# Sums of quarter weights made by VectorE as fillers of the order, in place of accumulating transfers in DRAM

## Chip, cores and metric

The kernel runs on one core of a Trainium2 chip. The metric is the device time of one execution in microseconds. The core has five engines with queues of their own, which run side by side and wait for each other by semaphores: TensorE (PE, matmuls), VectorE (DVE), ScalarE (ACT), GpSimd (POOL) and SyncE (SP). In this kernel SP and POOL also issue the DMA transfers, SP the loads and the transposing transfers, POOL most stores. The on-chip memory SBUF has 128 partitions; matmul results go to PSUM; everything else lies in DRAM.

## What is computed

One layer of a hybrid encoder for two groups of requests, 1024 prompt rows and 8 x 16 sample rows, 1152 tokens together, with a model width of 1024:

```python
mod = jax.nn.silu(c) @ w_ada + b_ada
shift, scale, gate = jnp.split(mod[:, None, :], 3, axis=-1)
h = rms_norm(x, norm_g) * (1 + scale) + shift
proj = h @ w_in
q, k, v, z_att, z_ssd, xbc, dt_raw, gates = jnp.split(proj, IN_SPLITS, axis=-1)
...
o_att, k_st, v_st = attn_fn(q, k, v)
att_branch = (o_att.reshape(b, s, ATT_WIDTH) * jax.nn.silu(z_att)) @ w_att_proj
xbc, conv_new = causal_dwconv(xbc, conv_buf, conv_w, conv_b)
xbc = jax.nn.silu(xbc)
...
y, h_new = ssd_scan(xs_h, dt, a,
...
y = (y + d_skip.astype(jnp.float32)[:, None] * xs_h).reshape(b, s, SSD_WIDTH).astype(x.dtype)
y = y * jax.nn.silu(z_ssd)
y = rms_norm(y.reshape(b, s, SSD_GROUPS, SSD_WIDTH // SSD_GROUPS),
             ssd_norm_g.reshape(SSD_GROUPS, SSD_WIDTH // SSD_GROUPS)).reshape(b, s, SSD_WIDTH)
ssd_branch = y @ w_ssd_proj
g_att, g_ssd = jnp.split(gates, 2, axis=-1)
merged = jax.nn.sigmoid(g_att) * att_branch + jax.nn.sigmoid(g_ssd) * ssd_branch
out = x + gate * (merged @ w_out)
```

There is attention over a band of chunks with 16 heads, and a state-space branch with 32 heads of 64 in 4 groups, scanned in chunks. The scan is float32 in the reference.

## The kernel before

**Stages.** All activations lie with channels on partitions and the 1152 tokens (`NT`) along the free dimension. Float32 products are made from float16 halves: a weight block is loaded as float32 into a `raw` buffer (line 672), ScalarE makes its high half (L690), VectorE its low half (L691), ScalarE sums its squares (L682), and three matmuls per block (L949, L950, L952) take high x high, high x low and low x high. The program is a list of items: eight units of attention (pairs of heads), then 16 pairs of state-space heads in 4 groups, then the gates, the attention projection, the two state-space projections and the output projection. The dense products of the state-space items run on PE while the attention's last units are still worked off, so the two stages overlap for some 150 us.

**The state-space stage.** A pair's dense part makes x (through `conv_gen`: ScalarE moves the product out of PSUM at L1783 and L1786, VectorE runs the convolution at L1806 and the gate multiply at L1812) and z (ScalarE L1964, VectorE L1965). `prelude` broadcasts rows of `acs_d` and `eacs_d` over partitions (L1980, L1984, loads on SP), loads the state (L1986) and builds decays on ScalarE (L1992, L1996). `main` turns x by a transposing DMA (L2017), unpacks it (L2019), scales it (L2024), runs the chunk products on PE (L2039, L2067, L2074, L2087) and stores y (L2104). At the last pair of a group PE sums squares over channels (L1368), for which VectorE adds the last square at L2127.

**Seven products in place of eight.** The second half of the gates and all later projections use a scheme with 7 products of quarter blocks in place of 8 (`quad_dense`, matmuls at L858 to L860). For each such block of weights with quarters a11, a12, a21, a22 it needs four sums besides: a21+a22, a21+a11, and two that build on the first. There are 20 of these blocks ("quads"). Before, the sums of four quads at a time are made by transfers alone (`quad_sums`, lines 693 to 712): two copies from the weights into the tensor `sum_d` in DRAM (L699, L700, on SP), four transfers on POOL's queue that add a quarter to what lies in DRAM (L698), and two copies within `sum_d` (L706, L710, on SP). Each moves 1 MB. The five batches are started at pairs 5, 7, 9, 11 and 13 of the item list (`SUMS`). The sums are loaded at L672 as pieces of a quad's job, beginning at 1303.6 us of the profile.

**What sets the order.** Generators first emit the whole program with a clock of their own (`pause` lets that clock pass); memory is handed out from an arena by layouts (`set_layout`). Then the class `Order` simulates the engines by a table of costs and gives each engine its final order: at each step the engine that is free first takes, among the instructions whose inputs are there, preferably those that are there with a margin, the one that was emitted earliest; nothing more than 1200 instructions ahead of the oldest open one is taken. On the chip each engine runs its list strictly in that order, so an instruction whose input is late holds up all behind it.

The choice in `Order.run` is this line:

```python
            u = min(sure or can, key=lambda u: u["i"])
```

Of the kernel before, what the change touches and what calls it, by code (L numbers as in the profile page):

```python
# [16 lines left out]
P = 128  # L17
# [122 lines left out]
class Order:  # L140
# [4 lines left out]
    SAFE_DMA = 2500.0  # L145
    SAFE_SLOT = 500.0
    AHEAD = 1200

    def __init__(self, tc, instructions, pinned, cuts, slow):
        self.tc, self.slow = tc, slow  # L150
        self.list = [x for x in instructions if x.opcode != "TilePoolBoundary"]
        self.pinned, self.cuts = pinned, cuts

# [76 lines left out]
    def build(self):  # L230
# [54 lines left out]
        for u in units:  # L285
            costs = [self.cost(x) for x in u["ins"]]
            u["busy"] = sum(c for c, _ in costs)
            u["lat"] = u["busy"] - costs[-1][0] + costs[-1][1]
            u["dma"] = u["ins"][0].opcode == "DMACopy" or u["ins"][0].opcode.startswith("DmaTranspose")
        self.tiles = tiles  # L290
# [23 lines left out]
    def run(self):  # L314
# [34 lines left out]
        while n < len(units):  # L349
            best = None  # L350
            for e in engines:
                lane = 0.0
                for u in ready[e]:
                    r, u["sure"] = u["r"], u["safe"]
                    for name in u.get("opens", ()):
                        s = slots[self.tiles[name][0]]
                        need = sum(self.tiles[o][0] == self.tiles[name][0] for o in u["opens"])
                        r = max(r, sorted(s)[need - 1] if len(s) >= need else 1e18)
                        u["sure"] = max(u["sure"], r + self.SAFE_SLOT)
                    u["now"] = r  # L360
                c = [u["now"] for u in ready[e] if u["i"] < low + self.AHEAD]
                if not c or min(c) > 1e17:
                    continue
                t = max(free[e], min(c))
                if best is None or t < best[0]:
                    best = (t, e)
            assert best, ("no unit can go on", [(e, [(u["i"], u["ins"][0].name) for u in ready[e]][:4]) for e in engines])
            t, e = best
            can = [u for u in ready[e] if u["now"] <= t and u["i"] < low + self.AHEAD]
            sure = [u for u in can if u["sure"] <= t]  # L370
            u = min(sure or can, key=lambda u: u["i"])
            ready[e].remove(u)
# [12 lines left out]
            if e == "PE":  # L385
                g = u["key"][1]
                if key[0] not in (None, g):
                    t += 70
                key[0] = g
            if e == "PE":  # L390
                log.append((t, t - free[e], u))
            start[u["i"]], finish[u["i"]] = t, t + lat
            free[e] = t + busy
            order[e].append(u)
            for name in u.get("uses", ()):
                x = self.tiles[name]
# [24 lines left out]
def trunk_kernel(ctx: ExitStack, tc: tile.TileContext, h, again):  # L421
# [32 lines left out]
    for n, w in PARAMS:  # L454
# [23 lines left out]
    bmask2 = cst[:, C_BM2:C_BM2 + 2]  # L478

    HN = NT // 2  # L480
    NSLOT = 12
    H0 = fixed[0] + 3 * 1024
    W0 = H0 + 16 * HN
# [14 lines left out]
    L_SSD = arena.set_layout(Z0, [("X", 1, XW), ("R", 2, 1184), ("t", 8, 36), ("pad", 1, 576), ("T", 9, NT), ("Y", 1, 1184), ("H", 1, 1024),  # L498
                                  ("g", 3, G3)])
    L_SSD["T"] = L_SSD["T"] + arena.set_layout(V0, [("T", 4, NT)])["T"]  # L500
    L_HEAD = dict(L_SSD, T=[x for x in L_SSD["T"] if x[0] + x[1] <= Z0 + 7 * NT])
    L_TAIL = arena.set_layout(Z0, [("T", 17, NT)])
    assert Z0 + 17 * NT + 2 * 384 <= E0
# [116 lines left out]
    dma = nc.sync.dma_start  # L620

    store = nc.gpsimd.dma_start
    pinned, cuts, slow = set(), set(), set()
    pinning = [True]

    def late(x):
# [63 lines left out]
            keep(nc.scalar.activation(hi, x, AF.Copy, scale=scale))  # L690
            keep(nc.vector.scalar_tensor_tensor(lo, x, scale, hi, ALU.mult, ALU.subtract))  # L691

    def quad_sums(i):

        b, s = batches[i], sum_d[i].rearrange("q p (s c) -> s p q c", c=512)
        x = h["quad"][2 * b[0] + NPLAIN:2 * b[-1] + 2 + NPLAIN].rearrange("(q o) p (e c) -> o e p q c", o=2, e=2)
        (a11, a12), (a21, a22) = ([x[o, e] for e in range(2)] for o in range(2))
        add = lambda out, x: nc.gpsimd.dma_start(out, x, accum_op=ALU.add)  # L698
        dma(s[0], a21)  # L699
        dma(s[2], a21)  # L700
        yield from pause(30000)
        add(s[0], a22)
        yield from pause(15000)
        add(s[2], a11)
        yield from pause(15000)
        dma(s[1], s[0])  # L706
        yield from pause(25000)
        add(s[1], a11)
        yield from pause(30000)
        dma(s[3], s[1])  # L710
        yield from pause(25000)
        add(s[3], a12)

    def quad_split(i):

        if i not in wsplit:
            bufs = []
            try:
# [3 lines left out]
                for b in bufs:  # L722
                    b.free()
                raise
            col = lambda k, e: slice((4 * e + k) * P, (4 * e + k + 1) * P)
            pick = {0: (bufs[0], bufs[1], col, 0, 0), 1: (bufs[0], bufs[1], col, 1, 1), 2: (bufs[5], bufs[6], col, 1, 1),
                    3: (bufs[2], bufs[2], col, 0, 1), 4: (bufs[3], bufs[4], col, 0, 0), 5: (bufs[3], bufs[4], col, 1, 1),
                    6: (bufs[5], bufs[6], col, 0, 0)}

# [79 lines left out]
        job(*(h["wall"][1 + 4 * u + i] for i in range(3)))  # L809
        job(h["wall"][4 + 4 * u])  # L810
    job(*(h["wlast"][i] for i in range(4)))
    SUMS = (5, 7, 9, 11, 13)
    NPLAIN = 8
    gate_w, at = [], 29
    for g in range(NG):
# [8 lines left out]
    for i in range(NPLAIN):  # L824
        job(gate_w[i])
    NQ_G = (16 - NPLAIN) // 2
    batches = [range(0, NQ_G)] + [range(NQ_G + 4 * i, NQ_G + 4 * i + 4) for i in range(4)]
    sum_d = [drp.tile([len(b), P, 2048], F32, name=f"sum{i}_d") for i, b in enumerate(batches)]
    for i, b in enumerate(batches):
        for j, q in enumerate(b):  # L830
            job(h["quad"][2 * q + NPLAIN], h["quad"][2 * q + 1 + NPLAIN], sum_d[i][j][:, :1024], sum_d[i][j][:, 1024:], quad=True)

    HT = NT // 2
    HC = NT // 4
# [1598 lines left out]
    for p in range(NPAIR):  # L2433
        g = p // PPG
        if p % PPG == 0 and p:
            items.append((group_dense(g, L_SSD), [], [group_lat(g)], 0.5))
        items.append(ssd(p))
        if p in SUMS:
            items[-1][1].append(quad_sums(SUMS.index(p)))
    items.append((gates_dense(), [h_pieces(), att_prep()], [], 0.5))  # L2440
    items.append((att_dense(), [tile_loads(4, ("ga", gate_d, 0)), ssd_prep(), mod_gate()], [], 0.5))
    items.append((ssd_dense(0), [], [], 0.5))
    items.append((ssd_dense(1), [tile_loads(3, ("acc", acc_d, 0), ("gs", gate_d, 8), ("att", att_o, 0))], [], 0.5))
    items.append((out_dense(), [], [], 0.5))
    run(items)
    order = Order(tc, list(nc.cur_bb.bb.instructions), pinned, cuts, slow)
    order.build()
    order.run()
    order.apply()
# [1867 lines left out]
```

## Time and profile before

| | us |
|---|---|
| runs, median of 3 | 1773.9 (1771.29 to 1774.73) |
| profiled execution, its own time | 1774.65 |
| its span | 1772.6 |
| PE busy | 1691.9 |
| VectorE busy | 1331.4 |
| ScalarE busy | 1060.8 |
| POOL busy | 369.6 |
| granted PE clock, mean over the span | 0.988 |
| attention, with PE nearly always busy | about 50 to 540 |
| attention's tail beside the first state-space pairs | 540 to 700 |
| state-space pairs | 700 to about 1265 |
| projections with seven products | about 1265 to 1772 |

Span and times are those of one execution seen by the hardware profiler. A row of the table by stretches gives start and end of the stretch and its length, then for PE, PE's weight loads, VectorE, ScalarE and POOL the busy us and in brackets the number of instructions, then the granted PE clock (1.00 is full speed), the mean busy share of the 16 DMA engines (it can come out above 1) and GB/s. A row of the timeline gives start, duration, engine, line and operation; in square brackets stands how long the engine was idle before it and whose result ended that. SPq rows are what SP issued.

### The profile page before, as it was taken

What the parts mean: (1) busy time and instruction counts of PE and PEld (TensorE: products, weight loads), DVE (VectorE), ACT (ScalarE), POOL (GpSimd) and SP (SyncE); (2) the same over time, 40 slices, a digit from 0 to 9 for tenths busy, and PEclk for the clock granted to TensorE, in tenths of its full rate; (3) what the DMA queues carried; (4) which work ended last, traced back from release to release, by engine and by line L of the source; (5) the groups of instructions that cost most, each with busy time, mean ns of one, the idle gap of its engine ahead of it and who ended that gap; (6) DMA issues with size and microseconds to landing.
All of it is one profiled execution on the core that took longest, in us unless ns stands there. A gap on an engine that the chain in (4) does not pass through costs nothing.

```text
span 1772.6 us, 36471 instructions
## 1 busy us (share of the span) xinstructions
PE 1691.9 (95%) x14265; PEld 1127.0 (64%) x14265; DVE 1331.4 (75%) x2466; ACT 1060.8 (60%) x2130; POOL 369.6 (21%) x620
## 2 busy tenths in 40 slices
PE   7999999999999898999899899999999999999896
PEld 3556656556555455666566566766667777777674
DVE  6468677777775855969778797886798587879952
ACT  8766556556565446654846575575579575775540
POOL 0233323323243011212322231221231000000000
PEclk9999999999999999999999999999999999999998
DMA  9248778888989999998987663556557785786651
GB/s 382 70 125 209 199 203 206 209 200 202 217 242 211 243 230 219 251 249 234 239 241 178 181 181 116 151 150 182 171 180 265 265 296 196 246 302 232 219 182 56
DMA packets 308703, 369.13 MB, mean 208 GB/s; under 512 B 211037, under 2 KB 212457, under 8 KB 308521
## 3 DMA queue, kind: packets, MB, share of 16 engines
q1 hardware_dynamic: 286696, 307.65, 61.5%
q0 software_dynamic: 21824, 59.06, 13.0%
q8 instruction: 114, 1.87, 0.4%
q14 instruction: 69, 0.56, 0.1%
HBM read 265.05 MB, written 95.04 MB: 203 GB/s over the span
## 4 chain that ended last, share of the span: by engine, by line
PE 52%; DMA 14%; DVE 14%; ACT 12%; issue 6%; POOL 1%; SPq 0%; DVEq 0%; ACTq 0%; POOLq 0%
PE d L949 7%; PE d L952 7%; PE d L950 7%; PE d L1002 5%; PE d L1004 5%; PE d L1003 5%; DMA arena<-in_wall_dram 4%; ACT arena L682 2%; PE g L1608 2%; ACT arena L1992 2%; DVE arena L691 2%; DMA arena<-arena 2%; DVE arena L2179 2%; DMA arena<-acs_d 2%; DVE arena L1806 1%
## 5 line engine op out<-in xcount | busy, mean ns | idle before, releaser
L949 PE MATMUL d<-arena 128*128 128x384 f16 x1320 | 435.2, 330 | 9.0 <-DVE arena L1965 6.3
L952 PE MATMUL d<-arena 128*128 128x384 f16 x1320 | 434.1, 329 | 0.6 <-DVE arena L691 0.6
L950 PE MATMUL d<-arena 128*128 128x384 f16 x1320 | 434.2, 329 | 0.0
L682 ACT ACTIVATE arena<-arena 128x1024 bf16<-128x1024 f32 (+4 forms) x217 | 199.2, 918 | 177.5 <-DMA arena<-in_wall_dram 134.0
L691 DVE SCALAR_TENSOR_TENSOR arena<-arena 128x1024 f16<-128x1024 f32 (+2 forms) x157 | 181.3, 1162 | 57.1 <-ACT arena L690 56.7
L949 PEld LDWEIGHTS <-arena 128*128 128x128 f16 x1320 | 130.3, 99 | 93.7 <-issue 17.8
L690 ACT ACTIVATE arena<-arena 128x1024 f16<-128x1024 f32 (+2 forms) x157 | 155.0, 993 | 53.5 <-DMA arena<-sum_d 31.5
L1002 PE MATMUL d<-arena 128*128 128x384 f16 (+1 forms) x568 | 186.8, 329 | 0.0
L950 PEld LDWEIGHTS <-arena 128*128 128x128 f16 x1320 | 130.2, 99 | 88.6 <-issue 13.1
L952 PEld LDWEIGHTS <-arena 128*128 128x128 f16 x1320 | 130.2, 99 | 88.5 <-issue 3.5
L1004 PE MATMUL d<-arena 128*128 128x384 f16 (+1 forms) x568 | 186.1, 328 | 0.0
L1003 PE MATMUL d<-arena 128*128 128x384 f16 (+1 forms) x568 | 186.1, 328 | 0.0
L1548 ACT ACTIVATE arena<-arena 128x640 f32<-128x640 f32 (+4 forms) x144 | 100.8, 702 | 66.8 <-DVE arena L1551 66.4
L859 PEld LDWEIGHTS <-arena 128*128 128x128 f16 x1120 | 109.5, 98 | 40.4 <-issue 13.1
L858 PE MATMUL d<-arena 128*128 128x288 f16 x440 | 125.8, 286 | 3.8 <-ACT arena L877 3.1
L860 PEld LDWEIGHTS <-arena 128*128 128x128 f16 x1120 | 109.5, 98 | 30.6 <-issue 2.7
L858 PEld LDWEIGHTS <-arena 128*128 128x128 f16 x1120 | 109.7, 98 | 29.2 <-issue 1.7
L859 PE MATMUL d<-arena 128*128 128x288 f16 x440 | 125.8, 286 | 1.1 <-DVE arena L2179 1.1
L860 PE MATMUL d<-arena 128*128 128x288 f16 x440 | 125.8, 286 | 0.0
L858 PE MATMUL s<-arena 128*128 128x288 f16 x360 | 102.9, 286 | 4.2 <-ACT arena L877 2.5
L1806 DVE SCALAR_TENSOR_TENSOR arena<-arena 128x1176 f32<-128x1176 f32 x72 | 103.7, 1440 | 3.1 <-ACT arena L1803 2.2
L1992 ACT ACTIVATE arena<-arena 128x128 f32<-128x128 f32 x288 | 90.0, 391 | 22.0 <-DMA arena<-acs_d 22.0
(277 smaller groups left out, 3493.9 us busy)
## 6 DMA issues: line engine op xcount, KB each, us to landing
arena<-in_wall_dram SPq DMA_DIRECT2D x77, 512.0 KB, 5.3
sum_d<-in_quad_dram POOLq DMA_DIRECT2D x20, 1024.0 KB, 13.9
arena<-in_quad_dram SPq DMA_DIRECT2D x40, 512.0 KB, 4.2
arena<-sum_d SPq DMA_DIRECT2D x40, 512.0 KB, 4.2
arena<-acs_d SPq DMA_DIRECT2D x32, 576.0 KB, 5.6
arena<-in_kc_dram SPq DMA_DIRECT2D x64, 256.0 KB, 4.0
arena<-in_vc_dram SPq DMA_DIRECT2D x64, 256.0 KB, 4.1
arena<-in_wada_dram SPq DMA_DIRECT2D x24, 512.0 KB, 9.4
```

The source lines that it names most:

```text
L682: keep(nc.scalar.activation(junk[:, :n], x, AF.Square, scale=scale * n ** -0.5, accum_out=sums[:, c:c + 1]))
L690: keep(nc.scalar.activation(hi, x, AF.Copy, scale=scale))
L691: keep(nc.vector.scalar_tensor_tensor(lo, x, scale, hi, ALU.mult, ALU.subtract))
L858: nc.tensor.matmul(ps, wh, xh[:, c], start=first and k == 0, stop=False, skip_group_check=not first)
L859: nc.tensor.matmul(ps, wh, xl[:, c], start=False, stop=False, skip_group_check=not first)
L860: nc.tensor.matmul(ps, wl, xh[:, c], start=False, stop=k == 3, skip_group_check=not first)
L949: nc.tensor.matmul(ps, hi.r[:, wc], kh.r[:, tok], start=k == 0, stop=False)
L950: nc.tensor.matmul(ps, hi.r[:, wc], kl.r[:, tok], start=False, stop=False)
L952: nc.tensor.matmul(ps, lo.r[:, wc], kh.r[:, tok], start=False, stop=k == nk - 1)
L1002: nc.tensor.matmul(ps, kh.r[:, tok], wh, start=k == 0, stop=False)
L1003: nc.tensor.matmul(ps, kh.r[:, tok], wl, start=False, stop=False)
L1004: nc.tensor.matmul(ps, kl.r[:, tok], wh, start=False, stop=k == KT - 1)
```

## The change

`quad_sums` now handles one quad. It takes two buffers of 1024 float32 columns (layout `L_SUM`, two slots at the end of the stage's area, just behind those of the state-space layout), loads the quad's two halves from the weights, lets VectorE add quarters in place four times, and stores both buffers in pieces of 2 KB to a `sum_d` tensor of its own on POOL's queue. The weights' first half of each quad is packed with its two quarters swapped, and `quad_split` picks its parts accordingly. The 20 quads are handed evenly to pairs 0 to 14 of the item list. The four additions are marked as fillers: in `Order.run` they count as emitted 600 instructions later than they are, so that other work that is ready goes ahead of them.

```diff
+    FILL = 600
...
+            u["at"] = u["i"] + self.FILL * (u["ins"][0].name in self.fill)
...
-            u = min(sure or can, key=lambda u: u["i"])
+            u = min(sure or can, key=lambda u: u["at"])
...
+    NSUM = 2
...
+    L_SUM = arena.set_layout(E0 - NSUM * 1024, [("s", NSUM, 1024)])
...
-    def quad_sums(i):
-
-        b, s = batches[i], sum_d[i].rearrange("q p (s c) -> s p q c", c=512)
-        x = h["quad"][2 * b[0] + NPLAIN:2 * b[-1] + 2 + NPLAIN].rearrange("(q o) p (e c) -> o e p q c", o=2, e=2)
-        (a11, a12), (a21, a22) = ([x[o, e] for e in range(2)] for o in range(2))
-        add = lambda out, x: nc.gpsimd.dma_start(out, x, accum_op=ALU.add)
-        dma(s[0], a21)
-        dma(s[2], a21)
-        yield from pause(30000)
-        add(s[0], a22)
-        yield from pause(15000)
-        add(s[2], a11)
-        yield from pause(15000)
-        dma(s[1], s[0])
-        yield from pause(25000)
-        add(s[1], a11)
-        yield from pause(30000)
-        dma(s[3], s[1])
-        yield from pause(25000)
-        add(s[3], a12)
+    def quad_sums(q):
+
+        x = yield from wpair(L_SUM, "s", 1024)
+        for o, b in enumerate(x):
+            dma(b.ap, h["quad"][2 * q + NPLAIN + o])
+        yield from pause(7000)
+        a12, a11, a21, a22 = (b.ap[:, c:c + 512] for b in x for c in (0, 512))
+        for out, a, b in ((a22, a21, a22), (a21, a11, a21), (a11, a22, a11), (a12, a11, a12)):
+            fill.add(nc.vector.tensor_tensor(out, a, b, ALU.add).ins.name)
+            yield from pause(900)
+        s = sum_d[q].rearrange("p (s o c) -> p s o c", o=2, c=512)
+        for o, b in ((1, x[0]), (0, x[1])):
+            store(s[:, :, o], b.ap.rearrange("p (s c) -> p s c", c=512))
+        stored(*x)
...
-    SUMS = (5, 7, 9, 11, 13)
...
-        if p in SUMS:
-            items[-1][1].append(quad_sums(SUMS.index(p)))
+        items[-1][1].extend(quad_sums(q) for q in range(NQUAD * p // 15, min(NQUAD, NQUAD * (p + 1) // 15)))
...
+    ar["quad"][::2] = np.roll(ar["quad"][::2], 512, 2)
```

In the changed program a line behind `quad_sums` has a number that is lower by 4 (before L2019, now L2015), and the loading line L672 is L676.

SP's queue at the passage from attention to the state-space stage, before. `acs_d` and `eacs_d` hold the running sums of the scan, `in_wall` weights, `in_vc` cached values, `in_quad` the quads' weights:

```order
L1881 DMA acs_d<-arena 32x1152
L1884 DMA eacs_d<-arena 32x1152
L1590 DMA_TRANSPOSE arena<-arena 128x10x128 x2
L710 DMA sum_d<-sum_d 128x4x512
L1727 DMA arena<-in_vc_dram 128x512 x4
L1980 DMA arena<-acs_d 128x1152
L1590 DMA_TRANSPOSE arena<-arena 128x10x128 x2
L706 DMA sum_d<-sum_d 128x4x512
L672 DMA arena<-in_wall_dram 128x1024
```

The same place in the changed program:

```order
L1880 DMA eacs_d<-arena 32x1152
L1586 DMA_TRANSPOSE arena<-arena 128x10x128
L1723 DMA arena<-in_vc_dram 128x512 x3
L676 DMA arena<-in_wall_dram 128x1024
L1723 DMA arena<-in_vc_dram 128x512
L1976 DMA arena<-acs_d 128x1152
L701 DMA arena<-in_quad_dram 128x1024
L1586 DMA_TRANSPOSE arena<-arena 128x10x128 x2
L1773 DMA arena<-in_sconv_dram 128x24
```

The copies within `sum_d` are gone, and the first load of a quad (L701) stands here, behind the first broadcast of `acs_d`; no transfer of the sums stands ahead of it any more. (The previous `sum_d` transfers of SP stood before these rows, in the attention's last units.) The last load of a quad stands next to the load of the last pair's state.

VectorE's queue where the first quad is added, before. `arena` is SBUF, names that begin with d or g are PSUM tiles:

```order
L1806 SCALAR_TENSOR_TENSOR arena<-arena 128x1176
L2019 COPY arena<-arena 128x2x1152
L1812 SCALAR_TENSOR_TENSOR arena<-arena 128x1024
L1813 SCALAR_TENSOR_TENSOR arena<-arena 128x128
L2024 TENSOR_TENSOR arena<-arena 128x1152 x2
L1806 SCALAR_TENSOR_TENSOR arena<-arena 128x1176
L1965 SCALAR_TENSOR_TENSOR arena<-arena,d_8500 128x384
```

And in the changed program:

```order
L1802 SCALAR_TENSOR_TENSOR arena<-arena 128x1176
L2015 COPY arena<-arena 128x2x1152
L705 TENSOR_TENSOR arena<-arena 128x512
L1808 SCALAR_TENSOR_TENSOR arena<-arena 128x1024
L1809 SCALAR_TENSOR_TENSOR arena<-arena 128x128
L2020 TENSOR_TENSOR arena<-arena 128x1152 x2
L705 TENSOR_TENSOR arena<-arena 128x512 x2
L695 SCALAR_TENSOR_TENSOR arena<-arena 128x1024
L705 TENSOR_TENSOR arena<-arena 128x512
L1802 SCALAR_TENSOR_TENSOR arena<-arena 128x1176
```

The four additions (L705) stand singly or in pairs between the pair's own work; at other quads all four stand in a row. Behind the last of them POOL's queue gets the two stores (L709).

More of the change, by code (lines that the diff above doesn't have):

```diff
@@ L147, with __init__ @@
     AHEAD = 1200
-    def __init__(self, tc, instructions, pinned, cuts, slow):
-        self.tc, self.slow = tc, slow
+    FILL = 600
+    def __init__(self, tc, instructions, pinned, cuts, slow, fill):
+        self.tc, self.slow, self.fill = tc, slow, fill
         self.list = [x for x in instructions if x.opcode != "TilePoolBoundary"]
@@ L622, in trunk_kernel @@
     store = nc.gpsimd.dma_start
-    pinned, cuts, slow = set(), set(), set()
+    pinned, cuts, slow, fill = set(), set(), set(), set()
     pinning = [True]
@@ L725, in quad_split @@
             col = lambda k, e: slice((4 * e + k) * P, (4 * e + k + 1) * P)
-            pick = {0: (bufs[0], bufs[1], col, 0, 0), 1: (bufs[0], bufs[1], col, 1, 1), 2: (bufs[5], bufs[6], col, 1, 1),
+            pick = {0: (bufs[0], bufs[1], col, 1, 1), 1: (bufs[0], bufs[1], col, 0, 0), 2: (bufs[5], bufs[6], col, 1, 1),
                     3: (bufs[2], bufs[2], col, 0, 1), 4: (bufs[3], bufs[4], col, 0, 0), 5: (bufs[3], bufs[4], col, 1, 1),
@@ L826, in trunk_kernel @@
     NQ_G = (16 - NPLAIN) // 2
[L827 to L831, printed above, removed]
+    NQUAD = NQ_G + 16
+    sum_d = [drp.tile([P, 2048], F32, name=f"sum{q}_d") for q in range(NQUAD)]
+    for q in range(NQUAD):
+        job(h["quad"][2 * q + NPLAIN], h["quad"][2 * q + 1 + NPLAIN], sum_d[q][:, 1024:], sum_d[q][:, :1024], quad=True)
     HT = NT // 2
@@ L2445, in trunk_kernel @@
     run(items)
-    order = Order(tc, list(nc.cur_bb.bb.instructions), pinned, cuts, slow)
+    order = Order(tc, list(nc.cur_bb.bb.instructions), pinned, cuts, slow, fill)
     order.build()
```

## The prediction

> **What bounds the kernel now.** I read the page's head first, then a table by stretches, then what TensorE (PE) waited for, then single gaps.
>
> ```profile
> span 1772.6 us, 36471 instructions
> PE 1691.9 (95%) x14265; PEld 1127.0 (64%) x14265; DVE 1331.4 (75%) x2466; ACT 1060.8 (60%) x2130; POOL 369.6 (21%) x620
> DMA  9248778888989999998987663556557785786651
> ```
>
> PE is busy for 95% of the span, so the end can only come earlier by PE's 80.7 us of idle time and by what a lowered clock costs it. The third line gives the DMA engines' busy share in 40 slices of 44.3 us: it stands at 8 or 9 in slices 6 to 22 and falls to 5 or 6 in slices 23 to 27. The table by stretches shows where PE's loss sits (columns: busy us of PE, weight loads, DVE, ACT, POOL, then granted clock, DMA share, GB/s):
>
> ```profile
> 540.00:700.00 160.00, 141.98 (x1257) 85.33 (x1246) 99.30 (x215) 82.36 (x164) 28.88 (x55) 0.96 1.09 230
> 700.00:920.00 220.00, 210.63 (x1641) 139.66 (x1640) 176.90 (x270) 129.50 (x245) 59.85 (x86) 0.98 0.96 244
> 920.00:1060.00 140.00, 131.72 (x980) 85.23 (x979) 115.00 (x171) 86.01 (x157) 35.16 (x54) 0.96 0.66 177
> 1060.00:1200.00 140.00, 138.67 (x1106) 93.17 (x1105) 117.22 (x180) 88.99 (x163) 31.15 (x52) 1.00 0.51 144
> 1200.00:1350.00 150.00, 150.00 (x1166) 102.30 (x1164) 122.78 (x180) 99.09 (x194) 32.73 (x50) 1.00 0.58 186
> ```
>
> PE loses 18.0, 9.4 and 8.3 us in the first three rows, 35.7 us together, and only 1.3 us in the last two, which are the same state-space stage. The transfers that make the sums in DRAM run from 525 to about 1003 us:
>
> ```profile
> L699 SPq DMA_DIRECT2D sum_d<-in_quad_dram x5: 592/631/712, 525.3 to 872.6; - x5
> L698 POOL DMA_DIRECT2D sum_d<-in_quad_dram x20: 1264/1344/2598, 561.1 to 990.8; - x20
> DMA to landing us min/median/max: 10.6/13.9/25.1
> ```
>
> (The three numbers with slashes are ns of one issue; "to landing" is that of L698.) So the loss and the sums share a stretch. That one makes the other has to be seen in single gaps. The timeline of the first large one, and of the last:
>
> ```profile
> 561.06 1.50 POOL L698 DMA_DIRECT2D sum_d<-in_quad_dram  x1
> 562.15 1.81 SPq L1732 DMA_TRANSPOSE arena<-arena  x1
> 579.49 0.88 DVE L1734 COPY arena<-arena 128x1280 uint16<-128x1280 uint16 x1 [7.46 <-DMA arena<-arena]
> 580.63 2.36 PE L1743 MATMUL g<-arena 128*32 128x128 f32 x40 [6.30 <-DVE arena L1734]
> ...
> 990.76 1.30 POOL L698 DMA_DIRECT2D sum_d<-in_quad_dram  x1
> 1003.48 1.06 ACT L682 ACTIVATE arena<-arena 128x1024 bf16<-128x1024 f32 x1 [10.87 <-DMA arena<-in_wall_dram]
> 1014.91 1.36 DVE L2127 TENSOR_TENSOR arena<-arena 128x1152 f32<-128x1152 f32 x1 [1.17 <-ACT arena L2105]
> 1016.42 1.50 PE L1368 MATMUL g<-arena 128*32 128x384 f32 x6 [4.77 <-DVE arena L2127]
> ```
>
> An accumulating transfer starts at 561.06; the transposing DMA issued 1.1 us later lands only before 579.49, so DVE's copy and then PE wait. At 990.76 the last one starts, a weight load behind it keeps ACT idle for 10.87 us, ACT's later work and DVE's L2127 slip, and PE waits 4.77 us. The same line L1368 in the quiet stretch:
>
> ```profile
> 1168.77 0.85 PE L1368 MATMUL g<-arena 128*32 128x384 f32 x6 [0.89 <-DVE arena L2127]
> ```
>
> There the wait is 0.89 us. Each gap also lowers the clock:
>
> ```profile
> 849.63 0.33 PE L950 MATMUL d<-arena 128*128 128x384 f16 x1
> 849.79 0.33 PE L952 MATMUL d<-arena 128*128 128x384 f16 x1
> 854.84 1.50 PE L1368 MATMUL g<-arena 128*32 128x384 f32 x6 [4.73 <-DVE arena L2127]
> 856.57 0.53 PE L950 MATMUL d<-arena 128*128 128x384 f16 x1
> 856.89 0.53 PE L952 MATMUL d<-arena 128*128 128x384 f16 x1
> ```
>
> Matmuls started 0.16 us apart before the gap and 0.32 us apart behind it. From the clock column the loss is at most 0.04 x 160 + 0.02 x 220 + 0.04 x 140 = 16.4 us, but part of the low clock lies in idle time that is already counted; I take 10 (an estimate).
>
> The Trainium skill, "TensorE: Matmul & The Clock Gate", section "What's actually happening", says that the clock halves after an idle window of about 3.4 us and returns after as long of steady work. The halved pitch agrees. By it, only the four gaps above 3.4 us would cost, 4 x 1.7 = 7 us, and the sum below would come 3 us later.
>
> **The change, part by part.** *Gain.* The 40 transfers of 1 MB go: 20 of L698 and 20 copies. What can come back is the idle time and the clock: 35.7 + 10 = **46 us**, and no more, since the rest of PE's idle time lies outside this stretch.
>
> *What stays of it.* The sums still cost transfers. The issues between 700 and 920 us, and a weight load in the quiet stretch from 1060 to 1200:
>
> ```profile
> sum_d<-in_quad_dram POOLq DMA_DIRECT2D x11, 1024.0 KB, 15.7
> arena<-in_wall_dram SPq DMA_DIRECT2D x14, 512.0 KB, 7.4
> sum_d<-in_quad_dram SPq DMA_DIRECT2D x6, 1024.0 KB, 8.2
> sum_d<-sum_d SPq DMA_DIRECT2D x6, 1024.0 KB, 11.8
> y_d<-arena POOLq DMA_DIRECT2D x5, 576.0 KB, 5.7
> ...
> arena<-in_wall_dram SPq DMA_DIRECT2D x10, 512.0 KB, 3.2
> ```
>
> The 23 sum transfers raised the share from 0.51 to 0.96 over 220 us: 99 us of all 16 engines, 4.3 us each, 172 us for 40. In their place come 40 loads and 40 stores of 512 KB. The quiet rows moved 144 GB/s at 0.51 and 186 at 0.58, so 282 to 321 GB/s of full use: 1.6 to 1.9 us each. From above, a lone load's whole 3.2 us bounds it. I take 1.75: 140 us, spread by the order from about 640 to 1250 us, 610 us, so +0.23 and a share of 0.74 in place of 0.96 (0.93 with 3.2 us). PE's loss at such a share lies between the quiet rows' 1.3 in 290 us (0.5%) and the third row's 8.3 in 140 (5.9%): over 610 us 3 to 36 us. That third row's gaps have sum transfers ahead of them, as shown, and the new pieces are half as large; so I take 2%, **12 us**. In the attention tail before 640 us no sum transfer is left at all.
>
> *Added to DVE.* 80 additions of 128x512 float32. The nearest rows, from 700 to 1250 us:
>
> ```profile
> L2093 DVE TENSOR_TENSOR arena<-arena 128x512 f32<-128x512 f32 x14 | 9.6, 684 | 0.1
> L2092 DVE TENSOR_TENSOR arena<-arena,g 128x512 f32<-128x512 f32 x14 | 9.5, 679 | 3.6 <-PE g L2087 3.6
> ```
>
> 80 x 0.684 = 54.7 us. In the quiet row DVE is idle for 22.8 of 140 us, 99 us at that rate over 610, so the additions fit, but they take over half of the slack. On PE's path they cost between nothing and all 54.7 us; a gain is excluded, since nothing that PE waits for becomes shorter by them. The order has at most four in a row, 2.7 us, and none of them may stand aside once DVE has reached it: a load that is late holds up what is queued behind (in the rows shown, the conv's multiply, the scaled copies and the bank evictions that PE waits for). Near the quiet rows' 0.89 us wait I take half of 2.7 at each of three group ends and as much for late loads: **5 us**.
>
> The Trainium skill, "SBUF — State Buffer", section "Who interferes with whom", speaks against the additions: a DVE instruction with two SBUF inputs and a GpSimd one that reads SBUF exclude each other. The first row above has two SBUF inputs, the second one from PSUM, and they take 684 and 679 ns, so no such cost shows. By the rule, with POOL busy for 22% of the quiet row, some 18 additions would wait about half a us each, 9 us of DVE, and at the same share of the path 1 us of the end.
>
> *Queues.* POOL loses 20 issues of 1.344 us and gains 40 like this:
>
> ```profile
> L2104 POOL DMA_DIRECT2D y_d<-arena x16: 537/538/563, 727.0 to 1301.4; - x16
> ```
>
> 26.9 against 21.5 us, and POOL is idle for three quarters of the time: nothing. A store waits for its addition, and a small memset for the next conv buffer stands behind it, long before it is used. SP loses 20 issues (0.631 us for the kind shown) and gains 40:
>
> ```profile
> L672 SPq DMA_DIRECT2D arena<-in_quad_dram x40: 328/333/422, 1265.0 to 1697.5; - x40
> ```
>
> At 0.333 us that is 13.3 against 12.6 us. The next quad's load waits on SP until the two buffers' stores have landed; load, additions and store take 7.4 + 2.7 + 5.7 = 16 us of the 30 us between quads, so I take nothing; if a store is late, the weight loads and the broadcasts behind it on SP are late as well. PE and ACT keep all instructions, and behind 1260 us no engine's order changes, so the rest moves as a block.
>
> *Sum:* -46 + 12 + 5 = -29 us. Against the profiled execution's own 1774.65 us (its span and 2 us around it; the median of the runs is 0.75 us less) **1746 us**.
>
> **Rivals.**
> (a) *DMA stays the limit.* Loads and stores collide with transposes and broadcasts as before. For it speaks the upper price, a share of 0.93; against it that a quiet weight load lands in 3.2 us. With 36 us in place of 12: 1770 us.
> (b) *The seam, not the sums.* The 18.0 us up to 700 us may belong to the end of attention, where little dense work covers its chains; then they and their 6 us of clock stay and 1774.65 - 22 + 12 + 5 = 1770 us comes out. Against it stands the transposing DMA of the first gap.
> (c) *DVE becomes the pace, slower.* In the quiet stretch 18 additions in 140 us bring DVE from 117.2 to 129.8 us busy, 93%; if its in-order queue then sets the evictions for PE, the additions count in full: 1774.65 - 46 + 12 + 54.7 = 1795 us. It decides the sign once more than 34 of the 54.7 us lie on the path.
> (d) *The change does not do what it says*: the fillers would stand ahead of urgent work. The order's rows have them between other work, and the cost is that of (c), whose chance includes it.
>
> **How the numbers follow.** Forecast 0.67, 1731 to 1760; (a) 0.12; (b) 0.11; (c) with (d) 0.10. The least time is 1774.65 - 46 = 1729. The range 1730 to 1770 holds the forecast and half of (a) and (b) together, and leaves out the upper halves and (c), 0.2. A measurement of this kernel tells about 0.2% (3.5 us) from no change, so below 1770.4 is faster: the forecast and most of (a) and (b) give 0.82; same 0.08; slower 0.10.
>
> **What would show it.** Right: PE's idle time in the attention tail and the state-space stage falls from 37 to about 15 us, the clock column there returns to 0.99 or more, the DMA share from 700 to 920 us falls to about 0.75, weight loads there land in under 5 us, the additions take about 0.68 us, and the stretch behind the state-space stage keeps its length. Wrong: PE waits for evictions or L2127 behind an addition (c), additions that wait for their loads, transposes that still take over 10 us without a sum transfer ahead (a), or gaps that stay before 640 us (b).

## The result

| | before | after |
|---|---|---|
| runs, median of 4 | 1772.6 us (1766.15 to 1774.73) | 1721.28 us (1719.24 to 1722.93) |
| profiled execution, its own time | 1774.65 | 1722.93 |
| its span | 1772.6 | 1721.0 |

The ratio of the medians is 0.9716, with an interval of 0.9688 to 0.9744: faster by 2.8%. The forecast was 1746 us with a range of 1730 to 1770, so the direction held, and the time lies below the range and even below the 1729 us that the prediction called the least possible.

The head of the profile after (span, busy time with share and number of instructions, DMA share in 40 slices of 43 us):

```profile
span 1721.0 us, 36673 instructions
PE 1677.3 (97%) x14265; PEld 1122.4 (65%) x14265; DVE 1378.6 (80%) x2546; ACT 1061.5 (62%) x2130; POOL 391.5 (23%) x640
DMA  9248789797988688686858767878658786777651
```

PE runs the same 14265 matmuls in 14.6 us less busy time, most of it the clock (see below), and its idle time fell from 80.7 to 43.7 us. The table by stretches of after, over the stretches that the prediction shows of before (same columns):

```profile
540.00:700.00 160.00, 158.41 (x1442) 99.15 (x1438) 130.78 (x261) 105.80 (x211) 31.06 (x56) 1.00 0.77 195
700.00:920.00 220.00, 219.40 (x1725) 146.38 (x1725) 195.44 (x301) 131.82 (x237) 57.31 (x97) 1.00 0.72 203
920.00:1060.00 140.00, 139.79 (x1060) 91.95 (x1058) 130.44 (x193) 86.98 (x164) 48.63 (x63) 1.00 0.76 227
1060.00:1200.00 140.00, 138.46 (x1102) 92.49 (x1101) 123.03 (x196) 89.19 (x171) 43.62 (x61) 1.00 0.82 241
```

Idle time of 18.0, 9.4, 8.3 and 1.3 us became 1.6, 0.6, 0.2 and 1.5 us, and the clock column is 1.00 throughout. Since work moved to earlier times, such rows say where gaps went, and not yet what the end gained. For that, cut both traces at the same events: the first seven-product matmul (1322.33 us before, 1275.50 after) and a point just behind the last matmul. Of before:

```profile
1322.33:1756.50 434.17, 420.74 (x3413) 331.17 (x3411) 335.87 (x495) 264.56 (x479) 33.59 (x58) 1.00 0.67 234
540.00:1322.33 782.33, 745.33 (x5917) 483.57 (x5906) 604.69 (x980) 458.41 (x867) 177.96 (x283) 0.98 0.79 200
```

And of after:

```profile
1275.50:1714.00 438.50, 421.79 (x3413) 331.87 (x3411) 340.20 (x500) 268.01 (x487) 36.43 (x60) 1.00 0.68 234
540.00:1275.50 735.50, 729.25 (x5897) 478.01 (x5893) 647.04 (x1052) 455.04 (x859) 197.05 (x300) 1.00 0.75 214
```

The stretch with the sums became 46.8 us shorter (30.7 of them PE's idle time, 16.1 its busy time), the projections 4.3 us longer, and what follows the last matmul went from 1772.6 - 1756.5 = 16.1 to 1721.0 - 1714.0 = 7.0 us: 9.1 us shorter. Together -51.6 us. (Up to 540 us and in the projections PE's busy time is 0.4 and 1.1 us longer; with these the 16.1 become the head's 14.6.)

The 9.1 us were in no step of the prediction. They stand in the groups of the kernel's last line, where every engine has instructions named DRAIN. POOL's three; of before (min, median and max ns, then first and last start):

```profile
L4299 POOLq DRAIN  x3: 50/107/8236, 1763.6 to 1772.4; - x3
```

and of after:

```profile
L4295 POOLq DRAIN  x3: 40/107/727, 1719.4 to 1720.8; - x3
```

The longest is the first of the three, from 1763.6 us before and from 1719.4 after. It takes 8.24 us before and 0.73 us after: 7.5 of the 9.1 us. It is called the long DRAIN below.

What the sums cost the DMA engines stands in the queues' part of the page. Of before (packets, MB, share of 16 engines):

```profile
q1 hardware_dynamic: 286696, 307.65, 61.5%
q0 software_dynamic: 21824, 59.06, 13.0%
```

and of after:

```profile
q1 hardware_dynamic: 281896, 307.65, 63.7%
q0 software_dynamic: 17024, 59.06, 9.4%
```

Both kernels move the same bytes in both queues, as the page counts them. The gain is none of bytes saved.

### The profile page after: what moved, and what is told of

Read it like the earlier page. It is cut to its first block, busy times and chain, and to the rows that moved or that the text cites. A ratio compares the mean times of both kernels' runs of the same rounds, so it can differ in the third digit from the quotient of the medians.

```text
span 1721.0 us, 36673 instructions
## 1 busy us (share of the span) xinstructions
PE 1677.3 (97%) x14265; PEld 1122.4 (65%) x14265; DVE 1378.6 (80%) x2546; ACT 1061.5 (62%) x2130; POOL 391.5 (23%) x640
## 3 DMA queue, kind: packets, MB, share of 16 engines
q0 software_dynamic: 17024, 59.06, 9.4%
## 4 chain that ended last, share of the span: by engine, by line
PE 51%; DVE 18%; DMA 11%; ACT 11%; issue 7%; POOL 1%; SPq 1%; DVEq 0%; ACTq 0%; POOLq 0%
PE d L945 6%; PE d L948 6%; PE d L946 6%; PE d L998 5%; PE d L1000 5%; PE d L999 5%; ACT arena L686 3%; PE g L1604 2%; DVE arena L2175 2%; DMA arena<-in_quad_dram 2%; DMA arena<-acs_d 2%; DVE arena L695 2%; DVE arena L1802 2%; ACT arena L1988 1%; DMA arena<-sum_d 1%
## 5 line engine op out<-in xcount | busy, mean ns | idle before, releaser
L945 PEld LDWEIGHTS <-arena 128*128 128x128 f16 x1320 | 129.2, 98 | 90.2 <-issue 13.3
L1802 DVE SCALAR_TENSOR_TENSOR arena<-arena 128x1176 f32<-128x1176 f32 x72 | 103.2, 1434 | 5.5 <-ACT arena L1799 3.8
L2175 DVE SCALAR_TENSOR_TENSOR arena<-arena 128x1152 f16<-128x1152 f32 (+1 forms) x72 | 87.4, 1219 | 21.9 <-ACT arena L2173 21.7
```

The lines of the kernel that those rows point to most:

```text
L945: nc.tensor.matmul(ps, hi.r[:, wc], kh.r[:, tok], start=k == 0, stop=False)
```

## The experiments

**1. No sums at all.** From before; the sums are not made, and the seven-product jobs load plain quarters in their place, so the output is that of other weights.

```diff
-            job(h["quad"][2 * q + NPLAIN], h["quad"][2 * q + 1 + NPLAIN], sum_d[i][j][:, :1024], sum_d[i][j][:, 1024:], quad=True)
+            job(h["quad"][2 * q + NPLAIN], h["quad"][2 * q + 1 + NPLAIN], h["quad"][2 * q + NPLAIN], h["quad"][2 * q + 1 + NPLAIN], quad=True)
...
-        if p in SUMS:
-            items[-1][1].append(quad_sums(SUMS.index(p)))
```

> The kernel before without any transfer of the sums; where the quads are used, each job loads the quad's two weight halves a second time in place of the sums (same bytes), so the four sums are left out of the result. Theory (the sums' transfers in DRAM cost the gaps): 1715 to 1726 us, PE idle from 540 us to the first seven-product matmul under 5 us, as after. If it is below 1716, the loads, additions and stores of the change still cost that difference. Rival (the changed order of the attention tail, not the transfers): no change in the gaps up to 700 us, about 1750 to 1765 us. For the last stretch: if accumulating or DRAM-to-DRAM transfers on POOL's queue make POOL's last DRAIN long (8.2 us before, 0.7 after), it is under 1 us here.

Measured 1717.06 us, ratio to before 0.9686 (0.9638 to 0.9733). Two stretches of its table:

```profile
540.00:700.00 160.00, 158.41 (x1446) 99.20 (x1438) 130.01 (x259) 106.87 (x213) 26.80 (x56) 1.00 0.71 180
540.00:1271.78 731.78, 728.88 (x5900) 478.31 (x5893) 604.24 (x978) 460.67 (x867) 155.39 (x262) 1.00 0.57 159
```

Without the sums the gaps before 640 us are gone as well: 1.6 us of idle time are left of 18.0 up to 700 us. That speaks against the seam of the stages, rival (b), but leaving the sums out also changes the order of the engines' lists, from about 540 us on; experiment 2, with the old order, decides. Up to the first seven-product matmul the sums cost before 782.33 - 731.78 = 50.6 us, and they cost after 735.50 - 731.78 = 3.7 us. The projections take 434.7 us here, 433.8 before and 438.2 after (to the last matmul's start), so they are 3.5 us longer with the new sums than without any. The last matmul starts at 1706.44 against 1713.66 us after: **7.2 us** is all that the new sums cost in these two profiles. This kernel's queues:

```profile
q1 hardware_dynamic: 276136, 286.67, 59.0%
q0 software_dynamic: 11264, 38.09, 6.1%
```

Shares times spans give 1118 us of all 16 engines here, 1321 before and 1258 after. So the sums took 203 us of them before (the prediction had 172) and take 140 after (it had 140).

**2. The same transfers without the addition.** From before; the four transfers of a batch copy and no longer accumulate, so `sum_d` holds plain quarters.

```diff
-        add = lambda out, x: nc.gpsimd.dma_start(out, x, accum_op=ALU.add)
+        add = lambda out, x: nc.gpsimd.dma_start(out, x)
```

> The kernel before with the 20 accumulating transfers on POOL's queue turned into plain copies of the same shape (the sums are then wrong: only the last quarter copied stays). If the mere 1 MB transfers make the gaps: PE idle from 540 to 1060 us stays at 25 us or more and the time at 1760 to 1772. If the accumulation (the read of what lies there) is what is slow: landing of these transfers falls from 13.9 to about 8 us, PE idle under 15 us, 1735 to 1750. POOL's last DRAIN: 8 us if it follows the number of packets of POOL's queue (21824 before), under 1 us if it follows the accumulation.

Measured 1748.12 us, 0.9861 (0.9814 to 0.9908). The last matmul starts at 1728.65 us, 27.5 before that of before and 22.2 behind that of experiment 1. VectorE, ScalarE, POOL and SP have the same instructions in the same order as before (their sequences in the two traces are equal), so of 49.7 us, 27.5 belong to the accumulation. The other 22.2 belong to the 1 MB transfers or to the order, which is another without sums; they are not separated. The attention's tail:

```profile
540.00:700.00 160.00, 154.72 (x1413) 96.77 (x1414) 116.93 (x243) 101.73 (x208) 28.04 (x59) 1.00 1.05 264
```

PE's idle time there falls from 18.0 to 5.3 us with nothing but the accumulation gone, so 12.7 us of it are no matter of the seam, and rival (b) is out. The issues of the sums, over the whole trace (count, size, median us to landing), and the software queue:

```profile
sum_d<-in_quad_dram POOLq DMA_DIRECT2D x20, 1024.0 KB, 8.5
...
q0 software_dynamic: 16704, 59.06, 9.5%
```

The same bytes land in 8.5 us in place of 13.9, and the queue's share falls from 13.0% to 9.5%. The long DRAIN takes 9.14 us, so it is not the accumulation that makes it long.

**3. The DRAM sums in small pieces.** From before, one quad to a batch: 256 KB a transfer, started in fours at the same pairs.

```diff
-    batches = [range(0, NQ_G)] + [range(NQ_G + 4 * i, NQ_G + 4 * i + 4) for i in range(4)]
+    batches = [range(i, i + 1) for i in range(20)]
...
-            items[-1][1].append(quad_sums(SUMS.index(p)))
+            items[-1][1].extend(quad_sums(4 * SUMS.index(p) + i) for i in range(4))
```

> The kernel before with the same sums made for one quad at a time: 160 transfers of 256 KB in place of 40 of 1 MB, started at the same five places, same bytes. If the size of a burst makes the gaps (a transpose or load behind 1 MB waits for it): gaps become shorter, 1740 to 1760. If the amount of DMA work does: same gaps, 1765 to 1785 with the further issues on POOL (80 x about 0.8 us more). POOL's last DRAIN stays at 8 us if it follows the accumulation or the packets.

Measured 1796.84 us, 1.012 (1.0085 to 1.0155), 1.2% slower than before. A row of its stretches (the profile is that of its fastest execution, 1779.4 us):

```profile
700.00:920.00 220.00, 199.20 (x1506) 130.41 (x1505) 170.53 (x252) 124.70 (x234) 82.93 (x111) 0.98 0.92 226
```

PE idles for 20.8 us where it idled for 9.4. A quarter of the bytes still took 9.9 us to land (median of 80). Cutting the bursts does not help; with four times as many transfers it is slower.

**4. The additions without their rank.** From after; they count as emitted where they are.

```diff
-    FILL = 600
+    FILL = 0
```

> The changed kernel with FILL = 0: the additions are ranked like other work. If the rank is what keeps the additions off PE's path: 1724 to 1735 with PE waits for evictions behind additions. If there is slack enough for them anywhere: 1719 to 1724, no difference.

Measured 1743.1 us, 0.9832 (0.9785 to 0.9879): 22 us slower than the change. Two rows of VectorE's timeline and one of PE's show a place:

```profile
1081.46 0.69 DVE L705 TENSOR_TENSOR arena<-arena 128x512 f32<-128x512 f32 x1 [3.03 <-DMA arena<-in_quad_dram]
1082.07 1.61 DVE L2044 SCALAR_TENSOR_TENSOR arena<-arena,g 128x64 f32<-128x64 f32 x8
...
1083.83 0.91 PE L2083 MATMUL g<-arena 128*128 128x128 f32 x6 [1.26 <-DVE arena L2044]
```

VectorE stands for 3.03 us at an addition whose load is late, L2044, which PE needs, is behind it, and PE waits 1.26 us. But this is the only one of the six PE gaps above 1 us between 700 and 1300 us with a late load in front; the longest, 3.83 us before 956.50, has two additions of 0.69 us between other work, and loads hold VectorE up at additions for 10.8 us in all here and for 15.1 after (row below), where PE idles for 6.3 us in all. So the rank is worth 22 us, and one way in which it acts is shown; most of the 22 us come with an order that is another as a whole, and are not traced.

**5. Twice the VectorE work.** From after; behind each addition a second instruction of the same size takes the maximum of the sum with itself, which changes nothing.

```diff
             fill.add(nc.vector.tensor_tensor(out, a, b, ALU.add).ins.name)
+            fill.add(nc.vector.tensor_tensor(out, out, out, ALU.max).ins.name)
```

> The changed kernel with each of the 80 additions followed by a second VectorE instruction of the same shape that leaves the values as they are (maximum of the sum with itself), also marked as a filler: 55 us more VectorE work. If VectorE had slack for the additions: 1721 to 1728 us. If the additions lie on PE's path in part, as the predicted 5 us said: 1726 to 1735. If VectorE is then the pace of the stage: 1745 or more, with VectorE above 95% from 700 to 1200 us.

Measured 1748.89 us, 0.9844 (0.9776 to 0.9912): 27.6 us for 55 us more work. What PE waits for between 540 and 1300 us (total, times, longest), and one stretch:

```profile
PE d L946 <- DVE arena L1962: 7.9, 3, 5.0
PE g L2036 <- DVE arena L2021: 4.2, 1, 4.2
PE g L2036 <- DVE arena L2120: 3.8, 1, 3.8
...
920.00:1060.00 140.00, 132.04 (x1039) 87.21 (x1038) 136.07 (x218) 81.07 (x150) 42.91 (x63) 0.98 0.71 212
```

Here, where PE loses most (8.0 us), VectorE is the pace: 136.07 of 140 us busy, and PE waits for its results. Rival (c) is a real mechanism whose point lies beyond the change: the first 55 us fit into the slack, of the next 55 half do not.

**6. The DRAM sums, spread.** From before; one quad to a batch, handed to pairs 0 to 14 as the change hands them out.

```diff
-    batches = [range(0, NQ_G)] + [range(NQ_G + 4 * i, NQ_G + 4 * i + 4) for i in range(4)]
+    batches = [range(i, i + 1) for i in range(20)]
...
-        if p in SUMS:
-            items[-1][1].append(quad_sums(SUMS.index(p)))
+        items[-1][1].extend(quad_sums(q) for q in range(20 * p // 15, min(20, 20 * (p + 1) // 15)))
```

> The kernel before with its sums made by transfers in DRAM, but for one quad at a time (256 KB per transfer, 160 transfers, same bytes) and handed to pairs 0 to 14 as the changed item list does. If even spreading is what made the gain: 1735 to 1755 us. If the work of the transfers is: 1765 to 1800, like the run with small pieces at the old places (1797), with the gaps spread over a longer stretch.

Measured 1800.35 us, 1.0162 (1.01 to 1.0225). That is as slow as the small pieces at the old places (experiment 3). The even spread, which the change has too, is not where the gain is from.

**7. Each load of a quad twice.** From after.

```diff
         for o, b in enumerate(x):
             dma(b.ap, h["quad"][2 * q + NPLAIN + o])
+            dma(b.ap, h["quad"][2 * q + NPLAIN + o])
```

> The changed kernel with each of the 40 quad loads issued twice into the same buffer: 20 MB more of plain loads, DMA share from 700 to 1200 us about 0.09 to 0.12 higher (about 0.85). If PE's loss grows steadily with the DMA share, as the prediction's 2% at 0.74 said: 1729 to 1740 us. If plain loads cost PE nothing below a full share: 1721 to 1727.

Measured 1761.09 us, 0.9944 (0.9914 to 0.9975): 40 us slower than the change. Its reading is not clean. The second load writes the same buffer, so it waits on SP until the first has landed, and SP's queue stands for that time:

```profile
SPq L702 <- DMA arena<-in_quad_dram: 74.9, 25, 8.2
```

These are 74.9 us of waits at the head of SP's queue between 640 and 1300 us, with all loads behind them. Such waits need not cost much: in the change itself, whose sums cost 7.2 us in all, SP stands for 103.2 us in the same stretch, at loads into buffers whose last sums are still being stored (total, times, longest, after):

```profile
SPq L701 <- DMA sum_d<-arena: 103.2, 25, 9.2
```

Whether the 40 us are SP's blocked queue or the 20 MB more can't be told from this run.

**8. The rank doubled.** From after, `FILL = 1200`.

> The changed kernel with FILL = 1200 in place of 600: the additions go still further behind other work. If a lower rank keeps helping: 1716 to 1720 us, near the run without sums (1717). If 600 already keeps them off the path: 1720 to 1724. If they then come so late that loads of the next quads and SP behind them wait: above 1725.

Measured 1783.72 us, 1.0057 (1.0028 to 1.0086), 0.6% slower than before. The stretch from 700 to 920 us has no idle time of PE at all; behind it stand two rows of VectorE's timeline and one of PE's, which show what follows:

```profile
700.00:920.00 220.00, 220.00 (x1730) 146.81 (x1729) 196.00 (x301) 133.61 (x237) 56.57 (x95) 1.00 0.68 200
```

```profile
1272.29 2.86 DVE L705 TENSOR_TENSOR arena<-arena 128x512 f32<-128x512 f32 x4
1288.78 2.87 DVE L705 TENSOR_TENSOR arena<-arena 128x512 f32<-128x512 f32 x4 [13.63 <-DMA arena<-in_quad_dram]
...
1330.00 0.40 PE L854 MATMUL d<-arena 128*128 128x288 f16 x1 [41.52 <-ACT arena L2173]
```

The last quads' additions slip behind the state-space stage, where only two buffers go round, and PE waits 41.5 us at the seam. Of the three ranks tried 600 is the best: against it 0 costs 22 us and 1200 costs 62.

**9 to 11. The drain at the end.** Three ways to store the sums, from after: all stores by SP, one of a quad's two by SP (the second buffer's), and each store in two halves on POOL.

```diff
-            store(s[:, :, o], b.ap.rearrange("p (s c) -> p s c", c=512))
+            dma(s[:, :, o], b.ap.rearrange("p (s c) -> p s c", c=512))
```

```diff
-            store(s[:, :, o], b.ap.rearrange("p (s c) -> p s c", c=512))
+            (store if o else dma)(s[:, :, o], b.ap.rearrange("p (s c) -> p s c", c=512))
```

```diff
-            store(s[:, :, o], b.ap.rearrange("p (s c) -> p s c", c=512))
+            for i in range(2):
+                store(s[:, i, o], b.ap[:, 512 * i:512 * i + 512])
```

> The changed kernel with all 40 stores of the sums issued by SP in place of POOL. POOL's queue then has 144 transfers, as in the run without sums. If POOL's last DRAIN goes with the number of POOL's transfers (144: 3.2 us, 164: 8.2 and 9.1, 184: 0.7 to 0.9, 224: 4.0 twice), it is about 3.2 us. On the time otherwise: if a store that waits on SP for its additions holds up the weight loads behind it: 1730 us or more; if SP has room: 1719 to 1725.

> The changed kernel with the 20 stores of the first buffer issued by SP and the other 20 by POOL: 164 transfers on POOL's queue, as before the change, and no transfer within DRAM. If the last DRAIN goes with the number of POOL's transfers: 8 to 9 us, and the span behind the last matmul is 16 us as before. If it went with transfers within DRAM or accumulation: under 1 us.

> The changed kernel with each store cut in two, 80 stores of 256 KB: 224 transfers on POOL's queue, same bytes and packets. If the last DRAIN goes with the number of transfers: 4.0 us; if with the packets: 0.7 to 0.9. POOL issues 40 x 0.54 = 22 us more; if POOL has room, the last matmul stays within 5 us of the changed kernel's 1713.7.

Measured 1729.98 us, 0.9738 (0.9687 to 0.9789); 1729.51 us, 0.9737 (0.9684 to 0.979); and 1738.1 us, 0.9797 (0.9739 to 0.9855). The second says most. Its last matmul starts at 1713.67 us, as after (1713.66), and yet it ends 6.9 us later by its span:

```profile
L4295 POOLq DRAIN  x3: 40/107/6198, 1720.9 to 1727.7; - x3
```

Of these 6.9 us, 5.5 are the longer DRAIN (6.20 against 0.73). The forecast from the number of POOL's transfers (8 to 9 us) missed. The first has 3.17 us; the third has 1.05 us, where 4.0 were expected by transfers and 0.7 to 0.9 by packets, and loses its time elsewhere: its profiled execution is 13.0 us longer than that of after, and its last matmul 12.5 us later.

**12. Before, once more.**

> The kernel before once more, unchanged, for the part behind the last matmul: if its length belongs to the program, the last DRAIN is 8 to 9 us again and the span ends 16 us behind the last matmul; if it varies from run to run, it is another number.

Measured 1770.66 us. POOL's DRAINs in this second profile:

```profile
L4299 POOLq DRAIN  x3: 50/107/8236, 1759.7 to 1768.5; - x3
```

The length of the long one is the same to the nanosecond. As far as two profiles show, it belongs to the program and not to the execution.

## Why the prediction was right in sign and wrong in size

**Right: the mechanism.** The sums in DRAM made the gaps: without their accumulation, in the same order, over half of the loss is gone (experiment 2), without the sums all but 2.9 us of idle time (experiment 1), and with the change all but 6.3. Most of the observables came as named: idle time of PE from 540 us to the projections fell from 37.0 to 6.3 us (15 forecast); the clock column stands at 1.00, the DMA share at 0.72 from 700 to 920 us (0.74 in the sum); no bound by VectorE shows; and the groups of the additions, with an instruction that reads PSUM beside it, are (after, 600 to 1260 us):

```profile
L705 DVE TENSOR_TENSOR arena<-arena 128x512 f32<-128x512 f32 x80 | 55.3, 691 | 16.0 <-DMA arena<-in_quad_dram 15.1
L2088 DVE TENSOR_TENSOR arena<-arena,g 128x512 f32<-128x512 f32 x16 | 10.8, 676 | 1.1 <-PE g L2083 1.1
```

An addition takes 691 ns, forecast 684. By the rule of the Trainium skill, "SBUF — State Buffer", section "Who interferes with whom", a VectorE instruction with two SBUF inputs and a GpSimd one that reads SBUF exclude each other; 691 against 676 ns leaves hardly room for a loss of VectorE here. What POOL may have lost was not looked at. Not as named: the stretch behind the state-space stage did not keep its length (the projections are 4.3 us longer, the end 9.1 shorter), and additions that wait for their loads, named as a sign of being wrong, are there for 15.1 us and cost PE little (6.3 us of idle time in all).

**Wrong, 1: "and no more, since the rest of PE's idle time lies outside this stretch".** The prediction took 46 us as a ceiling. Idle time outside the stretch can change too when the change touches what causes it: POOL's DRAIN behind the last matmul gave 7.5 us, the whole end 9.1. This put the time below the 1729 us called the least, and it is luck: nothing in the change aims at it. The change alters what goes through POOL's queue, and the prediction looked at that queue for its issue times alone.

**Wrong, 2: the clock, 10 us.** It was cut down from a bound of 16.4 because "part of the low clock lies in idle time that is already counted". Before has seven stretches at half clock between 540 and 1322 us, of 3.4 or 6.8 us each. Three of them, and the sum of the seven:

```profile
643.10:646.50 3.40, 3.40 (x19) 1.56 (x15) 1.52 (x6) 1.52 (x3) 0.00 (x0) 0.51 1.06 295
687.50:690.90 3.40, 3.40 (x12) 1.67 (x12) 3.09 (x5) 3.07 (x2) 0.00 (x0) 0.50 1.09 332
796.70:800.10 3.40, 3.40 (x12) 1.63 (x11) 3.40 (x4) 1.81 (x1) 1.48 (x3) 0.51 0.91 211
sum 30.60, PE 26.67 PEld 12.45 DVE 26.35 ACT 21.56 POOL 3.34; mean PE 3.81 PEld 1.78 DVE 3.76 ACT 3.08 POOL 0.48
```

PE is busy for 26.67 of these 30.6 us, and at half clock half of that is lost: 13.3 us. So little of the low clock lies in idle time. PE's busy time in the stretch falls by 16.5 us in experiment 1; the other 3 us are not accounted for. The rule of the Trainium skill's page "TensorE: Matmul & The Clock Gate", section "What's actually happening", gave 7 us from the four gaps above 3.4 us, farther off: the three stretches shown follow gaps of 3.1 us, of 3.1 and 2.2, and of 1.4. With the idle time (35.7 forecast; 37.0 - 2.9 = 34.1 by experiment 1) the first term was 50.6 us where the forecast had 46.

**Wrong, 3: the 12 + 5 us given back.** Experiment 1 measures them: 7.2 us together, half of it in the projections, which were to move "as a block". The DMA time of the new sums came out as forecast (140 us of 16 engines); the step that failed is "a share of 0.74 ... I take 2%". The loss does not follow the share: from 700 to 920 us PE idles for 0.6 us at a share of 0.72, and from 1060 to 1200 for 1.5 us at 0.82, while before it idled for 8.3 us from 920 to 1060 at 0.66. What did change is how soon the loads land. The issues from 700 to 920 us, after:

```profile
sum_d<-arena POOLq DMA_DIRECT2D x14, 512.0 KB, 4.3
...
arena<-in_wall_dram SPq DMA_DIRECT2D x16, 512.0 KB, 4.5
...
arena<-in_quad_dram SPq DMA_DIRECT2D x13, 512.0 KB, 5.4
arena<-arena SPq DMA_TRANSPOSE x7, 17.3
```

Weight loads land in 4.5 us in place of 7.4 (under 5 was forecast); with the plain 1 MB copies of experiment 2 they still took 7.2. The transposes of the same stretch of before:

```profile
arena<-arena SPq DMA_TRANSPOSE x7, 5.3
```

They became slower, 17.3 us, and without any sums (experiment 1) they take 14.2, yet PE idles for 0.6 and 0.9 us. "Transposes that still take over 10 us" was named as a sign of rival (a), and it was a poor sign. The 5 us for VectorE have no measurement of their own: the stretch with the sums is 3.7 us longer than in experiment 1, against 12 + 5. Their working, half of 2.7 at three group ends and as much again for late loads, also gives 8 us and not 5. SP's wait for the stores, taken at nothing, came to the 103.2 us of experiment 7 and lies within the 7.2.

Sum of the three: 46 forecast against 50.6, 17 against 7.2, and 9.1 for the end, less 0.9 us by which the projections of experiment 1 are longer than before: 4.6 + 9.8 + 9.1 - 0.9 = 22.6 us, the distance from the forecast's -29 to -51.6. (In the prediction's DMA row slices 6 and 22 stand at 7 and slice 25 at 3, not at 8 or 9 and 5 or 6; nothing in the sum hangs on it.)

**The rivals.** (a) did not come: PE idles for 1.5 us in 140 even at a share of 0.82. (b) is out by experiments 1 and 2. (c) did not happen, but experiment 5 shows it one doubling away. (d) did not come either: the rank of the fillers acts, and without it 22 us are lost (experiment 4).

**Open.** What the 20 MB of added loads cost apart from SP's blocked queue (experiment 7), how the 22 us that remain in experiment 2 divide between the plain 1 MB copies and the order, and by what the rank saves most of its 22 us. No other way of making the sums was faster than the change; experiment 1, which makes none, leaves some 7 us to any, as far as the last matmul goes.

## What to carry to other kernels

Look for work to move off a shared resource by the waits that it puts on others, not by its bytes: these two kernels move the same 59.06 MB through one queue, and their last matmuls are 42.5 us apart. Hand such work to an engine as a filler with a rank, and measure the rank: no rank cost 22 us here, and twice the rank made the last additions late and cost 62. And look at the very end of the trace before calling idle time elsewhere out of reach.

## What the hardware showed unexpectedly

The long DRAIN on POOL took between 0.73 and 9.14 us, and 8.24 in both profiles of before. With the software queue's packets of the whole kernel beside it: 11264 packets 3.17 us (experiments 1 and 9), 14144 6.20, 16704 9.14, 17024 0.73 (after), 17664 1.05, 21824 8.24 (both profiles of before), 22784 4.07 and 4.03 (experiments 3 and 6). The four further variants with after's 17024 packets (experiments 4, 5, 7 and 8) have 0.89. Up to 16704 it rises by about 1.1 ns a packet, then it falls back, and once more behind 21824. The number of transfers does not order them: experiments 3 and 11 have 224 each, with 4.07 and 1.05 us. What sets it stays open, so these 7.5 us may not come with the same change elsewhere.

An accumulating transfer of 1 MB within DRAM took 13.9 us to land and a plain one at the same place 8.5 us (medians of 20); the queue's share of the 16 engines was 13.0% with the one and 9.5% with the other, for the same bytes.
